# Eight raw-weight buffers in the down projections of a two-layer encoder, with the residual x kept in HBM meanwhile

## The chip, the cores and the metric

One core of a Trainium2 chip runs the whole program. The metric is device time in microseconds (us) of one execution, the median of several runs. A profiled execution gives a trace of every engine: TensorE (PE, with its weight loads as PEld), VectorE (DVE), ScalarE (ACT), GpSimd (POOL) and SyncE (SP), whose queue issues nearly all the DMAs here.

## The reference

A trunk of two layers on x of 256 tokens by 2048 features, all in float32. Each layer is a token mixer (attention) and a ConvGLU feed-forward, each with a norm before and after:

```
def conv_glu(h, w_up, conv_w, conv_b, w_down):
    u = h @ w_up
    gate, val = u[..., :D_FF], u[..., D_FF:]
    gate = depthwise_conv3(gate, conv_w, conv_b)
    return (jax.nn.gelu(gate, approximate=False) * val) @ w_down
...
        x = x + rms_norm(m, p['mix_post'])
        h = rms_norm(x, p['ffn_pre'])
        x = x + rms_norm(conv_glu(h, *p['ffn']), p['ffn_post'])
```

D_FF is 5632, so `w_down` is 5632 by 2048: 46 MB per layer. The change concerns `@ w_down` of both layers and the x that is added after it.

## The kernel before, in words

**Weights as a stream of chunks.** Every weight that the program needs is cut into chunks of 128 partitions by 1024 float32 (512 KB), listed once in the order of their use (`all_chunks`). `_load` (L122) takes a buffer with the tag `raw`, of which there are four, and issues the DMA on SP. `_split` (L130) makes of a raw chunk two matmul operands in float32r: ACT casts it (L149, the high part `whi`), DVE subtracts the high part from the raw one (L144, the rest `wlo`). Once DVE has done that, the raw buffer is free. `whi` and `wlo` have five buffers each. `weights()` (L163) hands out the next chunk; it splits up to the chunk after next and then asks for three loads more. A product of float32 precision is the sum of three float32r matmuls: high weight by high and by low activation (L1269, L1270 in the down projection), low weight by high activation (L1272).

**The order on each engine.** The code is written as one program with generators that are ticked between chunks (`now`, `tick`). A scheduler of the framework then lays out each engine's instructions in a fixed order, and puts in the waits. SP works through its queue in that order: an instruction that waits holds up all behind it.

**The feed-forward** (`ffn`, L1072). The up projection takes 176 chunks. Beside it `block_sums` (L1124) loads parts of `w_down`, forms differences of their blocks on DVE (L1130) and writes them back to HBM (tiles `b..`); they are used instead of plain blocks in a scheme that needs seven block products instead of eight (Strassen's). Its tiles are `st` and `g_last`.

**The down projection** (`down`, L1157) works in two halves h of 1024 output columns. Its list of items (`down_order`, L41) mixes two kinds. A *plain* item is one chunk of 512 KB with 12 matmuls. A *pair* p is four items j = 0 to 3: three chunks of 512 KB with 6 matmuls each (those of j = 1 and 2 come from the blocks in HBM, tile `b`) and one of 256 KB with 3. Half 0 has 9 pairs, half 1 has 11. In half 0, and in half 1 for the first three pairs, two plain items stand among a pair's items; from the fourth pair of half 1 on, one. The pairs' other operands are sums of tokens' blocks, made by `sums` (L1169) on DVE and ACT and kept in the tiles `seven`. Their homes are tiles that nothing else needs at that time: `xm0`, `xm1`, `xm2` (the input of the up projection), `st`, `gw`, `yf`, `misc`. In half 1 the temporary of `sums` itself takes a `raw` buffer.

After the last pair of each half, `done` adds up the results on DVE (tiles `m`, L1160), squares them on ACT (L331) and multiplies by the gains, which are loaded by `gain_row` (L420, tile `gb`, on SP). The last five plain items of half 1 are held back: all five are split first and then multiplied for one block of tokens and for the other (`HELD`). Then comes `crossing` (L446), which updates x and starts the next layer's mixer, or in layer 1 `tail` (L597), which writes the result.

The residual x lies in four tiles `x0` to `x3` of 128 by 1024 float32 for the whole program. In `ffn` they are read by `pre_norm` (L337) at its start, and then not before `crossing` or `tail`.

Of the kernel before, what the change touches and what calls it, by code (L numbers as in the profile page):

```python
# [2 lines left out]

# [1 line left out]

# [4 lines left out]
F32 = mybir.dt.float32  # L10
# [6 lines left out]
P = 128  # L17
# [40 lines left out]
class Model:  # L58
# [6 lines left out]
    def __init__(self, ctx, tc, a, out):  # L65
        self.tc, self.nc, self.a, self.out = tc, tc.nc, a, out
        self.soon, self.bg, self.running = [], deque(), []
        self.held = deque()
        self.gate, self.lead, self.led = (), None, 8
        pool = lambda name, **k: ctx.enter_context(tc.tile_pool(name=name, **k))  # L70
        self.const = pool("const", bufs=1)
        self.act = pool("act", bufs=1)
        self.wp = pool("wp", bufs=1)
        self.small = pool("small", bufs=2)
        self.ps = pool("ps", bufs=4, space=bass.MemoryType.PSUM)
        self.dram = pool("dram", bufs=1, space=bass.MemoryType.DRAM)
        self.blocks = {}


    def now(self, gen, after=()):  # L80
# [41 lines left out]
    def _load(self, i):  # L122
        if i >= len(self.chunks) or i in self.loaded or i < self.at or i in self.made:
            return
        src = self.chunks[i]() if callable(self.chunks[i]) else self.chunks[i]
        raw = self.wp.tile([P, 1024], F32, tag="raw", name="raw", bufs=4)[:, :src.shape[-1]]
        self.nc.sync.dma_start(out=raw, in_=src)
        self.loaded[i] = raw

# [33 lines left out]
    def weights(self, upto=None):  # L163

        i = self.at
        if upto is None:
            upto = i + (2 if self.lead else 3)
            self.follow()
        for j in range(i, upto):
            self._split(j)  # L170
        for j in range(upto, i + 6):
            self._load(j) if j < upto + 4 else None
        self.at += 1
        return self.made.pop(i)

# [896 lines left out]
    def ffn(self, layer, pre):  # L1072
        nc, tc = self.nc, self.tc
        with tc.tile_pool(name=f"ffn{layer}", bufs=1) as sp:
            self.room = sp
            xs = self.xhl
            x = lambda k: xs[k // 4][:, k % 4].rearrange("p a t -> p (a t)")
            gh = [sp.tile([P, 4, T], F32R, tag=f"gh{i}", name=f"gh{i}") for i in range(NFG - 1)]
            gl = [sp.tile([P, 4, T], F32R, name=f"gl{i}") for i in range(NFG - 1)]
            cw = lambda j, c: self.gain(f"l{layer}_conv_w", j * KF + c)  # L1080
            gw = sp.tile([P, 4, T], F32, tag="gw", name="gw", bufs=1)
            misc = sp.tile([P, 4, T], F32, tag="misc", name="misc", bufs=1)
            self.rb = misc[:, 0]
            norm = self.now(self.pre_norm(sp))
            blocks = None
            for gi in range(NFG):
                if gi == 1:
                    blocks = self.now(self.block_sums(layer, sp))
                pg = self.proj_t(KD, x, "acc", ROWS[layer] if gi == 0 else 0, gi == 0)
                self.finish(norm)  # L1090
                act = sp.tile([P, 4, T], F32, tag="yf", name="yf", bufs=1)

                def gates(ins=None, gi=gi, pg=pg, act=act):
                    for i in range(4):
                        c = 4 * gi + i
                        g = self.joined(gw[:, 2 + i % 2], gw[:, i % 2], pg[i])
                        if ins and i == 0:
                            with self.behind([ins]):
                                self.spread(sp)
                        y = act[:, i]  # L1100
                        nc.vector.tensor_tensor(out=g, in0=g, in1=self.rb, op=ALU.mult)
                        nc.scalar.activation(y, g, AF.Identity, scale=cw(1, c), bias=self.gain(f"l{layer}_conv_b", c))
                        nc.vector.scalar_tensor_tensor(out=y[:, 1:], in0=g[:, :T - 1], scalar=cw(0, c), in1=y[:, 1:],
                                                       op0=ALU.mult, op1=ALU.add)
                        nc.vector.scalar_tensor_tensor(out=y[:, :T - 1], in0=g[:, 1:], scalar=cw(2, c),
                                                       in1=y[:, :T - 1], op0=ALU.mult, op1=ALU.add)
                        nc.scalar.activation(y, y, AF.Gelu)

                if gi:
                    gates()  # L1110
                pv = self.proj_t(KD, x, "at", after=None if gi else gates)
                if gi == NFG - 1:
                    self.finish(blocks)
                    both = sp.tile([P, 2, 4, T], F32R, tag="g_last", name="g_last", bufs=1)
                    gh.append(both[:, 0])
                    gl.append(both[:, 1])
                for i in range(4):
                    u = self.joined(gw[:, 2 + i % 2], misc[:, 2 + i % 2], pv[i])
                    nc.vector.tensor_tensor(out=u, in0=u, in1=self.rb, op=ALU.mult)
                    nc.vector.tensor_tensor(out=u, in0=u, in1=act[:, i], op=ALU.mult)  # L1120
                    self.parted(gh[gi][:, i, :], gl[gi][:, i, :], u)
            self.down(gh, gl, 2 * layer + 1, pre)

    def block_sums(self, layer, sp):  # L1124

# [28 lines left out]
                yield  # L1154
            old = (job, new)

    def down(self, gh, gl, post, pre):  # L1157

        nc = self.nc
        add = lambda out, a, b, op=ALU.add: nc.vector.tensor_tensor(out=out, in0=a, in1=b, op=op)  # L1160
# [2 lines left out]
        seven, m, gains = [], [], []  # L1163
        many = PAIRS[0 if pre else 1]

        homes = [(self.act, "xm0", 2), (self.act, "xm1", 2), (self.act, "xm2", 2), (self.room, "st", 2),
                 (self.room, "gw", 1), (self.room, "yf", 1), (self.room, "misc", 1)]

        def sums(upto, small=False):  # L1169

# [40 lines left out]
        def added(h, at):  # L1211

            p1, p5, p6, p7 = at
            x = m[h]
            nc.scalar.copy(x[:, 0, 0], p1)
            add(x[:, 1, 0], p6, x[:, 0, 0])
            yield
            add(x[:, 0, 1], p7, x[:, 1, 0])
            add(x[:, 1, 0], p5, x[:, 1, 0])
            yield  # L1220
            add(x[:, 1, 1], p5, x[:, 0, 1])
            yield
# [10 lines left out]
        def done(h, o, first=None):  # L1233
            if first:
                yield from first
            for t in range(2):
                self.square_sums(ss[:, t, 2 * h + o:2 * h + o + 1], total(h, o, t))
                yield
                scaled(h, o, t)
                yield  # L1240
# [4 lines left out]
        for h in range(2):  # L1245
            items = down_order(h, many[h])
            units = [n for n, item in enumerate(items) if item[0] == "seven"]
# [15 lines left out]
            def products(i, t, w):  # L1263
                group = []
                while used and used[0][1][:2] == (i, t):
                    q, (_, _, b, x, blk) = used.popleft()
                    group.append((banks[b], *x(), slice(512 * blk, 512 * blk + 512), q == first[b], q == last[b]))
                for bank, xh, xl, c, start, _ in group:
                    mm(bank, xh, w[0][:, c], start=start, stop=False, skip_group_check=loose)  # L1269
                    mm(bank, xl, w[0][:, c], start=False, stop=False, skip_group_check=loose)  # L1270
                for bank, xh, _, c, _, stop in group:
                    ins = mm(bank, xh, w[1][:, c], start=False, stop=stop, skip_group_check=loose)  # L1272
                return ins if group else None

            for i in range(n):
                if i == units[0]:
                    banks += [self.psum("at") for _ in range(4)]
                w = self.weights()
                while items[i][0] == "seven" and len(seven) <= items[i][1]:
                    self.tick()  # L1280
                for t in range(2):
                    products(i, t, w)
                self.tick()
                if i == units[-1]:
                    m.append(self.act.tile([P, 2, 2, 512], F32, tag="xm2" if h else "xm3", name=f"m{h}"))
                    if h:
                        gains.append(self.gain_row(post, 3))
                    ended = self.now(done(h, 0, added(h, banks[4:])))
# [153 lines left out]
```

## Time and profile before

| What | us |
| --- | --- |
| median of 3 runs | 2122.31 |
| lowest and highest | 2117.88, 2123.18 |
| the profiled execution's own time | 2115.0 |
| its span, first to last instruction | 2113.2 |
| down projection of layer 0 in the trace | 819.8 to 1082.2 |
| down projection of layer 1 in the trace | 1838.7 to 2104.8 |

The granted TensorE clock is 0.997 of full speed over the span. All times of the trace are counted from the span's start. In the tables by stretch a column gives the busy time of an engine and, as x with a number, the instructions that touch the stretch; PEclk is the granted clock, then comes the busy share of the 16 DMA engines and the GB/s that they moved. Matmuls are pipelined: one of 512 columns is shown with 0.39 us, but the next begins before it ends.

### The profile page before, as it was taken

The numbers are of one execution on the slowest core, as the hardware profiler recorded it, in microseconds if no ns is written. First come the engines' busy times: TensorE is split into PE (matmuls) and PEld (weight loads), VectorE is DVE, ScalarE is ACT, GpSimd is POOL, SyncE is SP. The second block draws the span as 40 slices with busy tenths as digits, with TensorE's granted clock in tenths as the row PEclk, the third lists the DMA queues.
The fourth block names the chain that finished last, engine by engine and source line by source line (L and its number), as shares of the span: only waits on it lengthen the run. The fifth ranks groups of instructions, "written<-read, shape, count | busy, mean of one in ns | idle before, by whom it ended". The sixth has DMA issues, their size and how long they took to land.

```text
span 2113.2 us, 29789 instructions
## 1 busy us (share of the span) xinstructions
PE 2061.7 (98%) x10882; PEld 1734.5 (82%) x10882; DVE 1561.4 (74%) x2388; ACT 1159.2 (55%) x1817; POOL 0.2 (0%) x4
## 2 busy tenths in 40 slices
PE   9999999999999999998999999999999999999987
PEld 7888888888888888776678998888888888887655
DVE  6876758887787768675587875797888866785756
ACT  7654546555455555554465654664555655554543
POOL 0000000000000000000000000000000000000000
PEclk9999999999999999999999999999999999999999
DMA  9545576898998666777755435698999866577774
GB/s 329 173 153 169 164 208 225 326 337 318 321 320 266 184 195 191 250 241 245 242 189 178 140 123 191 204 317 314 319 328 328 307 193 191 175 244 251 235 231 173
DMA packets 143284, 501.37 MB, mean 237 GB/s; under 512 B 15905, under 2 KB 16417, under 8 KB 143137
## 3 DMA queue, kind: packets, MB, share of 16 engines
q1 hardware_dynamic: 142848, 499.19, 71.0%
q8 instruction: 85, 1.39, 0.3%
q14 instruction: 63, 0.51, 0.1%
q10 hardware_dynamic: 288, 0.28, 0.0%
HBM read 455.36 MB, written 44.04 MB: 236 GB/s over the span
## 4 chain that ended last, share of the span: by engine, by line
PE 79%; DMA 12%; DVE 5%; ACT 3%; issue 1%; ACTq 0%; DVEq 0%; SPq 0%
PE ps L223 30%; PE ps L225 15%; PE ps L208 8%; PE ps L206 8%; PE ps L207 8%; DMA raw<-in_w_down 7%; DMA raw<-b 5%; DVE wlo L144 4%; ACT whi L149 2%; PE ps L1272 2%; PE ps L1269 2%; PE ps L1270 2%; PE ps L633 1%; PE ps L292 1%; DVE m L1160 1%
## 5 line engine op out<-in xcount | busy, mean ns | idle before, releaser
L144 DVE TENSOR_TENSOR wlo<-raw,whi 128x1024 fp32r<-128x1024 f32 (+1 forms) x780 | 924.8, 1193 | 415.9 <-ACT whi L149 402.6
L149 ACT CAST whi<-raw 128x1024 fp32r<-128x1024 f32 (+1 forms) x780 | 796.2, 1027 | 690.1 <-PE ps L223 156.2
L223 PE MATMUL ps<-xhl,whi 128*128 128x512 f32 x2752 | 952.6, 394 | 0.0
L225 PE MATMUL ps<-xhl,wlo 128*128 128x256 f32 x2752 | 757.5, 277 | 0.0
L223 PEld LDWEIGHTS ps<-xhl,whi 128*128 128x128 f32 x2752 | 513.9, 188 | 117.1
L225 PEld LDWEIGHTS ps<-xhl,wlo 128*128 128x128 f32 x2752 | 516.5, 188 | 2.6
L1269 PE MATMUL ps<-whi,gh 128*128 128x512 f32 x440 | 177.2, 403 | 24.7 <-ACT whi L149 21.7
L1270 PE MATMUL ps<-whi,gl 128*128 128x512 f32 x440 | 172.7, 392 | 0.0
L1272 PE MATMUL ps<-wlo,gh 128*128 128x512 f32 x440 | 146.5, 407 | 9.9 <-DVE wlo L144 6.9
L1130 DVE TENSOR_TENSOR blocks<-blocks 128x512 f32<-128x512 f32 (+1 forms) x120 | 103.6, 865 | 69.2 <-DMA blocks<-in_w_down 49.2
L206 PE MATMUL ps<-whi,xhl 128*128 128x512 f32 x336 | 132.3, 395 | 1.5 <-ACT whi L149 1.5
L1269 PEld LDWEIGHTS ps<-whi,gh 128*128 128x128 f32 x440 | 83.0, 189 | 59.1 <-ACT whi L149 39.0
L207 PE MATMUL ps<-wlo,xhl 128*128 128x512 f32 x336 | 131.4, 391 | 0.0
L208 PE MATMUL ps<-whi,xhl 128*128 128x512 f32 x336 | 130.9, 391 | 0.1
L1272 PEld LDWEIGHTS ps<-wlo,gh 128*128 128x128 f32 x440 | 79.6, 189 | 47.1 <-DVE wlo L144 33.5
L206 PE MATMUL ps<-whi,oh 128*128 128x512 f32 x256 | 100.3, 392 | 0.0
L207 PE MATMUL ps<-wlo,oh 128*128 128x512 f32 x256 | 99.7, 390 | 0.0
L208 PE MATMUL ps<-whi,ol 128*128 128x512 f32 x256 | 99.7, 389 | 0.0
L296 ACT COPY gw<-ps 128x256 f32<-128x256 f32 x176 | 62.3, 369 | 67.8 <-DVE gw L297 23.9
L1270 PEld LDWEIGHTS ps<-whi,gl 128*128 128x128 f32 x440 | 83.1, 189 | 16.1
L206 PEld LDWEIGHTS ps<-whi,xhl 128*128 128x128 f32 x336 | 63.1, 188 | 14.0 <-ACT whi L149 1.8
L208 PEld LDWEIGHTS ps<-whi,xhl 128*128 128x128 f32 x336 | 62.9, 188 | 13.8 <-DVE xhl L687 0.7
(229 smaller groups left out, 2209.8 us busy)
## 6 DMA issues: line engine op xcount, KB each, us to landing
raw<-in_w_up SPq DMA_DIRECT2D x352, 512.0 KB, 5.0
raw<-in_w_down SPq DMA_DIRECT2D x136, 512.0 KB, 4.7
raw<-in_w_in SPq DMA_DIRECT2D x88, 512.0 KB, 4.3
blocks<-in_w_down SPq DMA_DIRECT2D x80, 512.0 KB, 6.8
b<-blocks SPq DMA_DIRECT2D x80, 512.0 KB, 7.5
raw<-b SPq DMA_DIRECT2D x80, 512.0 KB, 6.4
raw<-in_w_out SPq DMA_DIRECT2D x64, 512.0 KB, 4.2
raw<-in_w_down SPq DMA_DIRECT2D x40, 256.0 KB, 4.5
```

The source lines that it names most:

```text
L144: return nc.vector.tensor_tensor(out=lo[:, s], in0=raw[:, s], in1=hi[:, s].bitcast(F32), op=ALU.subtract)
L149: self.nc.scalar.copy(hi[:, s], raw[:, s])
L206: mm(ps, lh, rh, start=start, stop=False)
L207: mm(ps, lh, rl, start=False, stop=False)
L208: return mm(ps, ll, rh, start=False, stop=stop)
L223: ins = mm(out[i], hi[:, s[kk]], x(k), start=k == 0, stop=False, skip_group_check=opening)
L225: ins = mm(out[i][:, :T], lo[:, s[kk]], x(k)[:, :T], start=False, stop=k == nk - 1, skip_group_check=opening)
L296: self.nc.scalar.copy(b, ps[:, T:])
L1130: nc.vector.tensor_tensor(out=x[:, a:a + n], in0=x[:, b:b + n] if n > 512 else x[:, a:a + n], in1=x[:, a:a + n] if n > 512 else x[:, b:b + ...
L1269: mm(bank, xh, w[0][:, c], start=start, stop=False, skip_group_check=loose)
L1270: mm(bank, xl, w[0][:, c], start=False, stop=False, skip_group_check=loose)
L1272: ins = mm(bank, xh, w[1][:, c], start=False, stop=stop, skip_group_check=loose)
```

## The change

Two kinds of SBUF space get a second use during `down`.

- `_load` takes turns among eight buffers there: the four `raw` ones, and the tiles `x2`, `yf`, `x3` and `misc`, under the name `raw_more`. `weights()` asks for loads up to nine chunks ahead instead of five. Six items before the last pair's end in half 1 the list `self.more` is emptied, so that loads use the four `raw` buffers again.
- `x0` and `x1` become the first homes of the tokens' sums, one pair each; `yf` and `misc` are homes no more.
- x therefore leaves SBUF: after the first column group of the up projection four DMAs of 512 KB on SP write it to HBM (tile `x_kept`), and at the last item of half 1's last pair four DMAs read it back (`x_back`).

```
-        raw = self.wp.tile([P, 1024], F32, tag="raw", name="raw", bufs=4)[:, :src.shape[-1]]
+        turn = next(self.turns) % (4 + len(self.more))
+        if turn < len(self.more):
+            pool, tag = self.more[turn]
+            raw = pool.tile([P, 1024], F32, tag=tag, name="raw_more", bufs=1)
+        else:
+            raw = self.wp.tile([P, 1024], F32, tag="raw", name="raw", bufs=4)
+        raw = raw[:, :src.shape[-1]]
         self.nc.sync.dma_start(out=raw, in_=src)
...
-        for j in range(upto, i + 6):
-            self._load(j) if j < upto + 4 else None
+        for j in range(upto, i + 6 + len(self.more)):
+            self._load(j) if j < upto + 4 + len(self.more) else None
...
                 if gi == 1:
+                    kept = self.dram.tile([4, P, 2, 512], F32, name=f"x_kept{layer}")
+                    for c in range(4):
+                        nc.sync.dma_start(out=kept[c], in_=self.x[c])
                     blocks = self.now(self.block_sums(layer, sp))
...
-        homes = [(self.act, "xm0", 2), (self.act, "xm1", 2), (self.act, "xm2", 2), (self.room, "st", 2),
-                 (self.room, "gw", 1), (self.room, "yf", 1), (self.room, "misc", 1)]
+        homes = [(self.act, "x0", 1), (self.act, "x1", 1), (self.act, "xm0", 2), (self.act, "xm1", 2),
+                 (self.act, "xm2", 2), (self.room, "st", 2), (self.room, "gw", 1)]
+        self.more = [(self.act, "x2"), (self.room, "yf"), (self.act, "x3"), (self.room, "misc")]
+
+        def x_back():
+            for c in range(4):
+                self.x[c] = self.act.tile([P, 2, 512], F32, name=f"x{c}")
+                nc.sync.dma_start(out=self.x[c], in_=kept[c])
...
             for i in range(n):
+                if h and i == units[-1] - 6:
+                    self.more = []
+                if h and i == units[-1]:
+                    x_back()
```

The order of TensorE's instructions is the same. On ACT and DVE the sums of the first two pairs are cut in two, and the last ones come earlier. On SP the queue changes in three places. (In the rows a line number of the kernel stands first; those of the changed kernel are 8 to 21 higher: L135 is the load of a chunk, L1098 the store of x, L1184 its way back, L428 the gain row.)

The first place is SP at the start of layer 0's up projection, before:

```order
L127 DMA raw<-in_w_up 128x1024 x7
L420 DMA gb<-in_post 128x512
L127 DMA raw<-in_w_up 128x1024 x3
L1143 DMA blocks<-in_w_down 128x1024
L127 DMA raw<-in_w_up 128x1024
L1143 DMA blocks<-in_w_down 128x1024 x2
```

and now:

```order
L428 DMA gb<-in_post 128x512
L1098 DMA x_kept_3681<-x_296 128x1024
L1098 DMA x_kept_3681<-x_320 128x1024
L135 DMA raw<-in_w_up 128x1024
L1098 DMA x_kept_3681<-x_344 128x1024
L135 DMA raw<-in_w_up 128x1024 x3
L1098 DMA x_kept_3681<-x_370 128x1024
L1154 DMA blocks<-in_w_down 128x1024 x2
```

The four stores of x stand among the 8th to 11th chunk of the up projection, two of them ahead of the 8th, and the first blocks come behind them.

The second place is SP in layer 0's half 1, from the third to the fifth pair (`b_2` to `b_4`; an integer at a name's end only tells tiles apart), before:

```order
L127 DMA raw<-b_2_5967 128x1024 x2
L127 DMA raw<-in_w_down 128x1024
L127 DMA raw<-in_w_down 128x512
L127 DMA raw<-in_w_down 128x1024 x2
L127 DMA raw<-b_3_6163 128x1024 x2
L127 DMA raw<-in_w_down 128x512
L127 DMA raw<-in_w_down 128x1024 x2
L127 DMA raw<-b_4_6354 128x1024 x2
```

and now:

```order
L135 DMA raw<-b_2_5972 128x1024 x2
L135 DMA raw<-in_w_down 128x1024
L135 DMA raw_more<-in_w_down 128x512
L135 DMA raw_more<-in_w_down 128x1024 x2
L135 DMA raw_more<-b_3_6168 128x1024
L135 DMA raw<-b_3_6168 128x1024
L135 DMA raw<-in_w_down 128x512
L1184 DMA x_9735<-x_kept_3681 128x1024
L135 DMA raw<-in_w_down 128x1024 x2
L135 DMA raw_more<-b_4_6359 128x1024 x2
```

The loads come in the same order, four in `raw` and four in `raw_more` by turns, and the first quarter of x is read back here already: the scheduler has moved it up, and the second quarter (not shown) to just behind the sixth pair's first chunk. Both stand behind loads that cannot be issued before PE is through with the first and the second pair, whose sums their tiles held.

The third place is SP at the end of layer 0's half 1, before:

```order
L127 DMA raw<-b_10_7485 128x1024 x2
L127 DMA raw<-in_w_down 128x512
L127 DMA raw<-in_w_down 128x1024 x7
L127 DMA raw<-in_w_in 128x1024 x7
```

and now:

```order
L135 DMA raw<-b_10_7490 128x1024 x2
L135 DMA raw_more<-in_w_down 128x512
L135 DMA raw_more<-in_w_down 128x1024 x2
L135 DMA raw<-in_w_down 128x1024 x4
L1184 DMA x_9739<-x_kept_3681 128x1024
L1184 DMA x_9741<-x_kept_3681 128x1024
L135 DMA raw<-in_w_down 128x1024
L135 DMA raw<-in_w_in 128x1024 x7
```

The other two quarters of x stand ahead of the last chunk of `w_down` and of the next layer's first chunks. Their tiles `x2` and `x3` held the chunks of the last pair's last item and of the second plain item behind it, so each waits for that chunk's split.

More of the change, by code (lines that the diff above doesn't have):

```diff
@@ L2 @@
 from contextlib import ExitStack
+from itertools import count
 import numpy as np
@@ L77, in __init__ @@
         self.blocks = {}
+        self.more, self.turns = [], count()
     def now(self, gen, after=()):
@@ L1121, in ffn @@
                     self.parted(gh[gi][:, i, :], gl[gi][:, i, :], u)
-            self.down(gh, gl, 2 * layer + 1, pre)
+            self.down(gh, gl, 2 * layer + 1, pre, kept)
     def block_sums(self, layer, sp):
@@ L1155, in block_sums, with down @@
             old = (job, new)
-    def down(self, gh, gl, post, pre):
+    def down(self, gh, gl, post, pre, kept):
         nc = self.nc
```

## The prediction

> **What bounds the kernel now.** I read the page first, then the tables by stretch through both down projections, then who waits there, the chain of waits and the landing times of one stretch.
>
> ```profile
> span 2113.2 us, 29789 instructions
> PE 2061.7 (98%) x10882; PEld 1734.5 (82%) x10882; DVE 1561.4 (74%) x2388; ACT 1159.2 (55%) x1817; POOL 0.2 (0%) x4
> ```
>
> PE looks full at 98%, but its time per matmul is the pipelined one, so a slack PE still looks busy. The number of matmuls in a stretch tells more. By stretch, with PE's busy time and count first, and the granted clock, the DMA share and GB/s last:
>
> ```profile
> 830.00:860.00 30.00, 30.00 (x134) 24.82 (x134) 28.28 (x38) 17.30 (x19) 0.00 (x0) 1.00 0.78 239
> 820.00:870.00 50.00, 50.00 (x222) 41.36 (x222) 44.43 (x64) 29.07 (x35) 0.00 (x0) 1.00 0.67 212
> 870.00:940.00 70.00, 68.12 (x287) 52.43 (x285) 44.45 (x43) 36.75 (x41) 0.00 (x0) 1.00 0.81 262
> 940.00:964.00 24.00, 20.74 (x84) 15.23 (x85) 19.26 (x29) 14.13 (x20) 0.00 (x0) 1.00 0.68 209
> 964.00:1060.00 96.00, 87.26 (x343) 61.20 (x342) 53.98 (x50) 46.47 (x50) 0.00 (x0) 1.00 0.76 244
> 1060.00:1077.00 17.00, 13.86 (x53) 10.38 (x52) 15.19 (x21) 11.01 (x16) 0.00 (x0) 0.90 0.79 262
> 1889.00:1959.00 70.00, 66.36 (x278) 50.99 (x278) 41.26 (x39) 35.77 (x40) 0.00 (x0) 1.00 0.78 253
> 1959.00:1980.00 21.00, 17.39 (x72) 12.80 (x71) 18.71 (x31) 12.30 (x18) 0.00 (x0) 1.00 0.64 204
> 1980.00:2078.00 98.00, 88.20 (x342) 61.89 (x341) 54.60 (x51) 47.55 (x51) 0.00 (x0) 0.98 0.75 238
> 2078.00:2104.00 26.00, 21.78 (x86) 16.57 (x85) 18.55 (x28) 8.55 (x13) 0.00 (x0) 0.93 0.37 136
> ```
>
> A matmul counts where it touches a stretch, so the first row gives a pitch of (30 + 0.39)/134 = 0.227 us at full flow. What a stretch lost is its length plus 0.39 less 0.227 times its count. In layer 0 that is 0.0 for 820 to 870, then 5.2 (the rest of half 0), 5.3 (the changeover between halves), 18.5 (half 1's pairs) and 5.4 (its end), 34.4 us together; in layer 1 7.3, 5.0, 20.8 and 6.9, 40.0 us together. So some 74 us are to be had. In the longest stretch of layer 0 these waited (engine, for whom: us, times, longest; last SP's queue):
>
> ```profile
> ACT whi L149 <- DMA raw<-in_w_down: 22.4, 17, 2.3
> ACT whi L149 <- DMA raw<-b: 18.0, 15, 3.2
> PEld ps L1269 <- ACT whi L149: 14.4, 17, 1.7
> SPq L127 <- DVE wlo L144: 69.1, 50, 2.4
> ```
>
> PE waits for the cast, the cast for the load, and SP, which should issue the load, waits 69 of 96 us for DVE to free a raw buffer. That is a ring, and the chain of waits of that stretch, by line, goes round in it: 57% in loads, 28% in L144 and L149.
>
> ```profile
> by line: DMA raw<-b 32.4%; DMA raw<-in_w_down 24.2%; DVE wlo L144 15.7%; ACT whi L149 12.1%; PE ps L1269 5.4%; PE ps L1270 4.6%; PE ps L1272 4.4%; issue 2.6%; ACTq L149 0.4%; DVEq L144 0.1%
> L144 DVE TENSOR_TENSOR wlo<-raw,whi 128x1024 fp32r<-128x1024 f32 (+1 forms) x50 | 55.0, 1117 | 41.0 <-ACT whi L149 38.4 <-PE ps L1272 2.2
> L149 ACT CAST whi<-raw 128x1024 fp32r<-128x1024 f32 (+1 forms) x49 | 46.7, 970 | 50.0 <-DMA raw<-in_w_down 22.4 <-DMA raw<-b 18.0 <-PE ps L1270 6.4
> raw<-in_w_down SPq DMA_DIRECT2D x23, 512.0 KB, 4.6
> raw<-b SPq DMA_DIRECT2D x18, 512.0 KB, 6.5
> raw<-in_w_down SPq DMA_DIRECT2D x9, 256.0 KB, 5.5
> ```
>
> One turn of a buffer takes the mean landing, (23 x 4.6 + 18 x 6.5 + 9 x 5.5)/50 = 5.45 us, and a cast and a subtraction, 0.97 + 1.12: 7.5 us. Four buffers give a chunk every 1.9 us, and the stretch indeed took 96/50 = 1.92 us per chunk. PE at full flow needs five chunks (2.36 MB) per 33 matmuls, one every 1.50 us, or 315 GB/s. The ring of four is the bound.
>
> **The change part by part.** *Four more buffers.* Eight buffers at 1.50 us allow a turn of 12.0 us, of which 2.1 are the split: loads may land after 9.9 us instead of 3.9. Whether the DMAs then carry 315 GB/s is the next question. This stretch of the up projection is the nearest row:
>
> ```profile
> 440.00:480.00 40.00, 40.00 (x233) 34.96 (x232) 35.94 (x57) 22.65 (x35) 0.00 (x0) 1.00 0.91 331
> ```
>
> They moved 331 GB/s at a share of 0.91, so some 364 at a full one (my estimate from this row). Half 1's pairs need 315, and with the two early quarters of x (1.05 MB in about 60 us) 333, or 91% of that. It is tight, but seven chunks of stock, about 10 us of PE's work, cover swings. DVE's five splits for a group are 5 x 1.12 = 5.6 of PE's 7.5 us, ACT's casts less, so both go on hiding behind PE. I count 90% of the loss of the pairs as won: 0.9 x (5.2 + 7.3) = 11.2 and 0.9 x (18.5 + 20.8) = 35.4 us. The bounds are 100% and what a rival below leaves.
>
> *The changeover.* SP stands still there for the gain rows (first row), and PE for a bank that DVE's additions free (second row):
>
> ```profile
> SPq L420 <- DVE m L1160: 4.3, 1, 4.3
> PE ps L1269 <- DVE m L1160: 1.3, 1, 1.3
> ```
>
> The first wait stays, but eight buffers cover 4.3 us, and the gain rows stand some chunks later. The second stays, at about 2 us per layer with its weight load. Won: 10.3 - 4 = 6.3 us, between 0 and 8.
>
> *The end of half 1.* DVE's fixed order puts six additions and gains between two splits (layer 1, DVE, then PE):
>
> ```profile
> 2086.26 1.22 DVE L144 TENSOR_TENSOR wlo<-raw,whi 128x1024 fp32r<-128x1024 f32 x1
> 2087.39 2.48 DVE L1160 TENSOR_TENSOR m<-ps,m 128x512 f32<-128x512 f32 x4
> ...
> 2091.76 2.35 DVE L144 TENSOR_TENSOR wlo<-raw,whi 128x1024 fp32r<-128x1024 f32 x2
> ```
>
> ```profile
> 2093.03 1.22 PE L1272 MATMUL ps<-wlo,gh 128*128 128x512 f32 x2 [3.84 <-DVE wlo L144]
> ```
>
> The fifth of the seven last chunks is thus split at 2093.0, and PE stands until then. That order stays; but it began late, since the splits ahead of it waited for loads. With early loads DVE starts about 0.8 us after the last pair, has seven additions and gains and two splits to do, some 7.6 us, and is through at 8.4. PE by then has two plain items (12 matmuls, 2.72 us each) and two of the held ones for one block of tokens (6 matmuls, 1.36 us each) behind it and needs that split two thirds into the next, at 9.1. I count 8 of 12.3 us as won, between 3 and 12. In both last stretches the clock column stands under 1: 17 us at 0.90 are 1.7 us lost, which this sum holds. The Trainium skill, TensorE: Matmul & The Clock Gate, What's actually happening, says that PE's clock is halved after an idle window of about 3.4 us and stays so for at least another. The trace agrees: a mean of 0.90 over 17 us is one window of 3.4 us at half. By that rule a stall at the end that stays, but gets shorter than a window, gives back its 1.7 us all the same.
>
> *x leaves and returns.* The four stores of a layer take at most 4 x 512 KB at 331 GB/s, 6.3 us of DMA time. The first two can go once x is updated, and SP issues its next chunk later than that anyway (DVE, then SP):
>
> ```profile
> 330.21 1.42 DVE L455 SCALAR_TENSOR_TENSOR x<-m,postr,x 128x512 f32<-128x512 f32 x2
> 334.63 5.27 SPq L127 DMA_DIRECT2D raw<-in_w_up  x3
> ```
>
> So the queue isn't held up. The 8th chunk, issued at 334.63, is needed after four chunks more of PE's work (about 11 us); this is the cover, and without it each store would cost 1.6 us. I take 0.5 us per layer, between 0 and 6.3. The first two reloads are in the 333 GB/s above. The last two stand ahead of the last chunk of `w_down` and make it 3.2 us later; it is needed 5.4 + 4 x 1.36 = 10.9 us after the last pair, and its load is early by then. Again 0.5 us per layer, between 0 and 3.2. A gain is excluded, since they only add traffic.
>
> *The sums.* Cutting the first two in halves adds a few short instructions where PE lost nothing (820 to 870); DVE has 5.6 us left there. Nothing; about 1 us if it hadn't. `yf` and `misc` are read last by DVE here:
>
> ```profile
> 826.43 0.76 DVE L682 TENSOR_TENSOR g_last<-misc,g_last 128x256 fp32r<-128x256 f32 x2
> ```
>
> The loads into them, and all behind, wait until 827.2 in layer 0. The earliest chunk so placed is the seventh of layer 1, which PE reaches 15 us after the stage's start and which can be issued after 8: nothing.
>
> *The sum.* 11.2 + 35.4 + 6.3 + 8.0 - 2.0 = 58.9 us, from 2115.0 to 2056.1 for an execution like the profiled one. The median of the runs is 7.3 us above that one, so I predict 2122.3 - 58.9 = 2063.4 us, say 2063.
>
> **The rivals.** *The DMAs become the bound.* For it: loads from `b` land after 6.5 us against 4.6, so blocks may be slow to read, and no stretch of the down projections exceeds 262 GB/s. Against it: DMA share there is 0.64 to 0.81, and 4 buffers can't ask for more. With 275 GB/s in the pairs, half 1's 23.4 MB (96 us at 244) and 1.05 MB more would take 88.9 us, a gain of 7.1; layer 1's 98 us become 88.7, a gain of 9.3; half 0's stretches gain 3.3 and 5.6. With 7 us at changeovers and ends and 2 us of costs: 2122.3 - 30.3 = 2092.
>
> *It costs time.* If loads land later just as they get more, so that the down projections keep their 244 GB/s, nothing is won and 2.1 MB of reloads come on top of a stage that the DMAs bound: 8.6 us per layer, 2139 us. It decides below 244 x (1 + 2.1/23.4) = 266 GB/s in half 1. For it: landing times with one to three loads in flight are already above this row of the up projection without blocks (min, median, max):
>
> ```profile
> DMA to landing us min/median/max: 3.2/4.2/4.6
> ```
>
> Against it: the same engines carry 331 GB/s with blocks and stores beside the weights.
>
> *The buffers are not what is short.* A lone load lands in 3.2 us; with that, four buffers turn in 5.3 us and feed 1.3 us per chunk, and PE's loss would come from elsewhere, or the scheduler's queue wouldn't issue the loads earlier: 2122 us. The 1.92 us per chunk, which the ring gives to 2%, speaks against it. The Trainium skill, DMA: Bandwidth & Descriptors, Anatomy of one DMA, has about 2.0 us plus the bytes at 436 GB/s for the path that GpSimd issues, 3.2 us for 512 KB, and by it four buffers would suffice as well. The trace agrees for a lone load only, not for those of the ring.
>
> **How the numbers follow.** Forecast 0.75; DMAs the bound 0.12; no effect 0.03; slower 0.05; all 74 us won, below 2050, 0.05. The forecast's own range is 2050 to 2080: at the low end all losses but one wait at each changeover are won (-72), at the high end 90% becomes 70% and the costs reach 6 us. To hold 8 in 10, with something kept back for what I don't see, the range is 2050 to 2092. A measurement of this kernel can tell about 0.3% (6 us) from no change. Faster 0.91 (forecast, all won, most of the DMA rival), same 0.04, slower 0.05.
>
> **What would show it.** Right: in half 1 SP's wait for L144 falls to a small part, the stretch's DMA rate rises to about 315 to 335 GB/s at a share over 0.9, and its 343 matmuls take about 80 us; DVE's additions at the end start before 1 us has passed and no stall of 3 us follows; the clock stays at 1.00 there. Wrong: landing times over 10 us with PE still waiting for casts (the DMAs are the bound), PE waiting in the up projection's first 40 us (the stores cost), or SP waiting long at the reloads of x (L1184).

## The result, and the profile after

| | us |
| --- | --- |
| before, median of 4 runs (2112.36 to 2123.18) | 2120.1 |
| after, median of 4 runs (2060.65 to 2063.37) | 2063.2 |
| ratio, 95% interval | 0.973, 0.9705 to 0.9763 |
| profiled execution after: own time, span | 2060.65, 2058.9 |
| down projections after, layer 0 and layer 1 | 832.2 to 1059.0, 1823.9 to 2050.1 |

The change makes the kernel 2.7% faster, at the time that was predicted; that the number fits is luck, as is shown below. The stretches of the down projections that answer to those shown of before (PE's busy time and count first; clock, DMA share and GB/s last):

```profile
882.00:946.00 64.00, 64.00 (x285) 53.01 (x284) 45.97 (x46) 36.98 (x42) 0.00 (x0) 1.00 0.87 291
946.00:966.00 20.00, 20.00 (x90) 16.58 (x89) 15.94 (x21) 14.05 (x19) 0.00 (x0) 1.00 0.82 256
966.00:1044.00 78.00, 78.00 (x346) 64.63 (x345) 57.12 (x56) 48.10 (x53) 0.00 (x0) 1.00 0.90 312
...
1956.00:2034.00 78.00, 78.00 (x346) 64.62 (x345) 54.88 (x51) 47.39 (x51) 0.00 (x0) 1.00 0.91 308
2034.00:2051.00 17.00, 16.49 (x70) 12.55 (x69) 14.24 (x25) 4.93 (x10) 0.00 (x0) 1.00 0.25 92
```

By the formula of the prediction (length plus 0.39 less 0.227 times the count) these lost nothing: 78 + 0.39 - 0.227 x 346 is -0.2. Half 1's pairs took 96 us for 343 matmuls before and take 78 for 346 now. The clock stands at 1.00 at the end too, where it was 0.90 and 0.93. Who still waits in the pairs of layer 0, all rows, and behind that SP's first row for 960 to 1040:

```profile
ACT whi L157 <- PE ps L1287: 29.2, 39, 2.1
DVE wlo L152 <- ACT whi L157: 18.4, 19, 1.8
```

```profile
SPq L135 <- DVE wlo L152: 54.9, 47, 2.6
```

No wait of PE is left, and none of ACT for a load: ACT waits for PE now, to hand back a cast's buffer. SP still waits 55 of 80 us for a raw buffer, though. A queue that runs ahead of its user always ends up waiting for a free buffer; that wait alone doesn't tell a ring that bounds from one that is full.

From its first matmul's start to its last one's, a down projection takes 226.8 and 226.2 us; before, it took 262.0 and 265.7 (819.8 to 1081.8, 1838.7 to 2104.4). That is 35.2 + 39.5 = 74.7 us won. The span fell by 2113.2 - 2058.9 = 54.3 us only: layer 0's down projection starts 12.4 us later, and from its last matmul to the first one of layer 1's it is 764.9 us instead of 756.9. These 20.4 us were lost in the two up projections. The same stretch of layer 0, before and then after:

```profile
580.00:660.00 80.00, 80.00 (x463) 69.95 (x463) 69.34 (x109) 43.38 (x67) 0.00 (x0) 1.00 0.91 320
```

```profile
580.00:660.00 80.00, 76.42 (x420) 65.20 (x419) 61.19 (x95) 39.35 (x61) 0.00 (x0) 0.98 0.90 310
```

This is where `block_sums` works beside the up projection (the block phase). DVE and PE waited there, from 480 to 660 us, for these (the rows of before are the first fence; PE has none in it):

```profile
DVE blocks L1130 <- DMA blocks<-in_w_down: 17.6, 5, 6.0
DVE blocks L1130 <- DMA raw<-in_w_up: 3.3, 1, 3.3
```

```profile
DVE blocks L1141 <- DMA blocks<-in_w_down: 18.3, 7, 4.2
DVE blocks L1141 <- DMA raw<-in_w_up: 8.1, 2, 4.3
DVE blocks L1141 <- issue: 7.8, 2, 6.2
PEld ps L233 <- DVE wlo L152: 6.7, 7, 2.7
PE ps L233 <- DVE wlo L152: 4.5, 5, 2.4
```

DVE, which works in order, stands 34.2 us at block sums whose data isn't there, instead of 20.9, and the splits that PE needs stand behind them. SP's queue from 440 to 660 us, before and after, at its block loads (L1143, L1154) and block stores (L1149, L1160):

```profile
SPq L1143 <- DMA b<-blocks: 15.6, 6, 4.3
SPq L1149 <- DVE blocks L1130: 0.9, 1, 0.9
```

```profile
SPq L1154 <- DMA b<-blocks: 16.3, 5, 8.0
SPq L1160 <- DMA blocks<-in_w_down: 8.2, 3, 3.5
SPq L1160 <- DVE blocks L1141: 6.1, 3, 2.1
```

SP now comes to stores of blocks before their sums are made, and stands there for 14.3 us with weight loads behind it. The longest wait of PE, and what stood before it on SP and DVE:

```profile
625.99 0.42 SPq L1154 DMA_DIRECT2D blocks<-in_w_down  x1
```

```profile
633.24 1.23 DVE L1141 TENSOR_TENSOR blocks<-blocks 128x1024 f32<-128x1024 f32 x1 [3.66 <-DMA blocks<-in_w_down]
...
637.30 1.22 DVE L152 TENSOR_TENSOR wlo<-raw,whi 128x1024 fp32r<-128x1024 f32 x1
```

```profile
638.57 0.53 PE L233 MATMUL ps<-xhl,wlo 128*128 128x256 f32 x1 [2.38 <-DVE wlo L152]
```

The block load that SP issued at 625.99 us landed at 633.2. DVE stood 3.66 us at the block sum that needs it, went through the instructions that its order has behind that sum, and came to the split only at 637.30, although the cast of that chunk was done by 631.0. PE waited for this split. After that SP stands for 8 us, from 630.3 to 638.4, at the next block load, which waits until the store just ahead of it has landed, and issues no weights; no wait of PE follows from this (from 640 to 830 us there is none). Just ahead of that block load stand two early loads of the down projection, at 629.16 and 629.98 us: x2 and x3 are free as soon as they are stored, so the scheduler may issue the first loads into them some 200 us before their use.

### The profile page after: what moved, and what is told of

Its sections match the earlier page's. It is cut to its first block, busy times and chain, and to the rows that moved or that the text cites. A ratio compares the mean times of both kernels' runs of the same rounds, so it can differ in the third digit from the quotient of the medians.

```text
span 2058.9 us, 29791 instructions
## 1 busy us (share of the span) xinstructions
PE 2037.1 (99%) x10882; PEld 1746.5 (85%) x10882; DVE 1560.2 (76%) x2388; ACT 1156.4 (56%) x1817; POOL 0.2 (0%) x4
## 4 chain that ended last, share of the span: by engine, by line
PE 87%; DVE 5%; DMA 4%; issue 2%; ACT 1%; SPq 0%; DVEq 0%; ACTq 0%
PE ps L231 25%; PE ps L233 12%; PE ps L216 8%; PE ps L214 8%; PE ps L215 8%; PE ps L1287 7%; PE ps L1286 7%; PE ps L1289 7%; DMA blocks<-in_w_down 3%; DVE wlo L152 2%; PE ps L641 1%; PE ps L300 1%; DMA raw<-in_w_up 1%; DVE blocks L1141 1%; PE ps L544 1%
## 5 line engine op out<-in xcount | busy, mean ns | idle before, releaser
L152 DVE TENSOR_TENSOR wlo<-raw,whi 128x1024 fp32r<-128x1024 f32 (+1 forms) x663 | 793.7, 1205 | 298.7 <-ACT whi L157 292.2
L157 ACT CAST whi<-raw 128x1024 fp32r<-128x1024 f32 (+1 forms) x663 | 682.9, 1036 | 520.7 <-PE ps L231 184.2
L233 PEld LDWEIGHTS ps<-xhl,wlo 128*128 128x128 f32 x2752 | 519.8, 189 | 15.6 <-DVE wlo L152 12.8
L1286 PE MATMUL ps<-whi,gh 128*128 128x512 f32 x440 | 171.5, 390 | 0.0
L152 DVE TENSOR_TENSOR wlo<-raw_more,whi 128x1024 fp32r<-128x1024 f32 (+1 forms) x117 | 130.7, 1132 | 48.6 <-ACT whi L157 43.8
L157 ACT CAST whi<-raw_more 128x1024 fp32r<-128x1024 f32 (+1 forms) x117 | 113.2, 979 | 77.2 <-PE ps L1287 70.0
L1289 PE MATMUL ps<-wlo,gh 128*128 128x512 f32 x440 | 138.8, 390 | 0.0
```

What stands on the lines that cost most here:

```text
L152: return nc.vector.tensor_tensor(out=lo[:, s], in0=raw[:, s], in1=hi[:, s].bitcast(F32), op=ALU.subtract)
L157: self.nc.scalar.copy(hi[:, s], raw[:, s])
L233: ins = mm(out[i][:, :T], lo[:, s[kk]], x(k)[:, :T], start=False, stop=k == nk - 1, skip_group_check=opening)
```

## The experiments

Three explanations of the 20.4 us were to be told apart. *Theory 1*: the stores of x make the scheduler lay out the block phase in another order on SP, and that order stalls DVE. *Theory 2*: the two early loads into x2 and x3 push the rest back. *A third*: the bytes of the stores and early loads cost it, wherever they are. The measurements of all runs together (excess is what a down projection took beyond full flow: of each step over 0.25 us from one of its matmuls' start to the next, the part beyond 0.227; SP's and DVE's waits for blocks are those of 440 to 660 and 480 to 660 us; each ratio is against runs of the kernel before made in the same rounds, whose medians are 2114.7 to 2120.1):

| kernel | median, us | ratio, 95% | SP at block stores | DVE at block sums | down 0 starts | down 0 to down 1 | excess, layers 0, 1 |
| --- | --- | --- | --- | --- | --- | --- | --- |
| before | 2120.1 | | 0.9 | 20.9 | 819.8 | 756.9 | 35.1, 38.5 |
| after | 2063.2 | 0.9705 to 0.9763 | 14.3 | 34.2 | 832.2 | 764.9 | 1.2, 0.6 |
| stores and reads of x, four buffers | 2141.0 | 1.0087 to 1.0135 | 17.0 | 29.5 | 832.6 | 768.5 | 39.7, 38.8 |
| early loads held back | 2060.0 | 0.9723 to 0.976 | 15.2 | 28.3 | 831.8 | 770.5 | 1.0, 0.3 |
| stores of x late | 2044.4 | 0.9637 to 0.9673 | 0.9 | 21.5 | 825.4 | 756.9 | 1.6, 0.0 |
| six buffers | 2041.8 | 0.9642 to 0.9679 | 0.9 | 20.7 | 819.9 | 757.7 | 1.4, 0.0 |
| five buffers | 2063.1 | 0.9728 to 0.9758 | 0.9 | 20.8 | 819.9 | 757.6 | 11.9, 10.2 |
| block stores held back | 2040.0 | 0.962 to 0.9649 | 0 | 6.0 | 819.9 | 757.0 | 1.1, 0.5 |
| stores of x by ScalarE | 2051.9 | 0.9672 to 0.9709 | 16.7 | 27.2 | 828.7 | 761.2 | 1.0, 0.3 |
| the hold alone, four buffers | 2115.5 | 0.9956 to 0.9999 | 0 | 3.7 | 820.1 | 756.9 | 36.8, 39.4 |
| the hold with six buffers | 2039.9 | 0.9617 to 0.9652 | 0 | 1.7 | 820.2 | 757.0 | 1.1, 0.0 |

**Stores and reads of x alone**, in the kernel before:

```diff
                 if gi == 1:
+                    kept = self.dram.tile([4, P, 2, 512], F32, name=f"x_kept{layer}")
+                    for c in range(4):
+                        nc.sync.dma_start(out=kept[c], in_=self.x[c])
...
+                if h and i == units[-1]:
+                    x_back()
```

> The kernel before, with the four stores of x to HBM at the second group of the up projections and the four reads back at the end of the down projections, but with four raw buffers and the old homes of the sums. Both down projections should flow as before (excess 35 and 38 us). Theory 1, the stores at the head of the block phase put SP's block loads, block stores and weight loads in another order and VectorE, which works in order, waits for late block loads: the up projections lose 8 to 16 us of the 20 that the changed kernel lost, total 2128 to 2137, ratio 1.004 to 1.008. Theory 2, the two loads into x2 and x3 that are issued in the middle of the block phase push the others back: nothing is lost here, ratio 0.999 to 1.001.

Theory 1's direction, and more than it gave: 1.1% slower than before, with 12.8 and 11.6 us lost in the up projections and 4.6 more in layer 0's down projection. It isn't quite the stores alone: the scheduler put two of the reads of x into the block phase too.

**The early loads held back**, in the changed kernel (`behind` makes the scheduler lay out an instruction behind those named):

```diff
-        self.nc.sync.dma_start(out=raw, in_=src)
+        with self.behind([self.last] if self.more else []):
+            self.last = self.nc.sync.dma_start(out=raw, in_=src)
```

> The changed kernel, with each raw load of the down projections held behind the raw load before it in SP's order, so that no load into x2 or x3 is issued in the block phase; the stores of x stay where they are. Theory 2 (those two loads push the others back): the jumps of 4.3 and 4.2 us at the end of the block phase go, with the drift behind them at most all 20 us; 2046 to 2055 us, ratio 0.965 to 0.969. Theory 1 (the order that the stores of x set): less than 3 us is won, ratio 0.972 to 0.974.

Theory 2 falls. The loads into x2 and x3 are gone from the block phase (the first one of layer 0 now comes at 831.7 us), and layer 0's loss is 12.0 instead of 12.4 us; layer 1's is 13.6 instead of 8.0.

**The stores of x late**, behind the block phase:

```diff
-        self.nc.sync.dma_start(out=raw, in_=src)
+        self.last = self.nc.sync.dma_start(out=raw, in_=src)
...
-                if gi == 1:
+                if gi == 9:
                     kept = self.dram.tile([4, P, 2, 512], F32, name=f"x_kept{layer}")
-                    for c in range(4):
-                        nc.sync.dma_start(out=kept[c], in_=self.x[c])
+                    with self.behind([self.last]):
+                        for c in range(4):
+                            nc.sync.dma_start(out=kept[c], in_=self.x[c])
+                if gi == 1:
                     blocks = self.now(self.block_sums(layer, sp))
```

> The changed kernel, with the four stores of x issued in the tenth group of the up projections, after the block phase, so that the block phase's order on SP is that of the kernel before, and the loads into x2 and x3 come after it too. Eight raw buffers in the down projections as in the changed kernel. Theories 1 and 2 both expect that the up projections lose nothing (under 3 us a layer) and the down projections keep their 226 us: about 2113 less 74.7 and plus 2 to 5, which is a total of 2042 to 2048, ratio 0.963 to 0.966. A third theory, that the bytes of the stores and of the early loads cost this wherever they stand, expects no change against the changed kernel, ratio 0.972 to 0.974.

As theories 1 and 2 had it, but for one thing. The bytes are all there, and most of the 20 us is back. Layer 0 still starts its down projection 5.6 us late, where under 3 were expected, without any wait of PE; the last section comes back to that.

**Six buffers**, two tiles of x stored:

```diff
-                    for c in range(4):
+                    for c in range(2):
                         nc.sync.dma_start(out=kept[c], in_=self.x[c])
...
-        self.more = [(self.act, "x2"), (self.room, "yf"), (self.act, "x3"), (self.room, "misc")]
+        self.more = [(self.room, "yf"), (self.room, "misc")]
...
-            for c in range(4):
+            for c in range(2):
                 self.x[c] = self.act.tile([P, 2, 512], F32, name=f"x{c}")
...
-                if h and i == units[-1] - 6:
+                if h and i == units[-1] - 4:
```

> Six raw buffers in place of eight: the two tiles of the up projections alone, which come free only at their end; x2 and x3 stay in SBUF, and x0 and x1 alone are stored and read back. By the ring's rule six turns at 1.50 us leave 9.0 us for landing, cast and subtraction, so landings up to 6.9 us are covered; the changed kernel's landings are 5.2 to 6.0 us on average. I expect an excess of 2 to 8 us in each down projection (before 35 and 38, with eight 1). The rival, that single landings scatter so far that eight are needed, gives an excess above 12 us each. The up projections: by theory 2 they lose nothing, by theory 1 half to all of what they lost. Total by ring's rule and theory 2: 2046 to 2058, ratio 0.965 to 0.971; with theory 1: 2055 to 2075, ratio 0.970 to 0.979.

Six do what eight do, and a little better than expected. Landings from 950 to 1032 us (of the issues, the 512 KB chunks of the down projection; each row ends with a median):

```profile
raw<-in_w_down SPq DMA_DIRECT2D x16, 512.0 KB, 6.2
raw<-b SPq DMA_DIRECT2D x12, 512.0 KB, 5.8
raw_more<-in_w_down SPq DMA_DIRECT2D x8, 512.0 KB, 5.8
raw_more<-b SPq DMA_DIRECT2D x4, 512.0 KB, 6.2
```

All these stay under the 6.9 us that six turns allow. Two stores of x, where four stood, don't upset the block phase.

**Five buffers**, the tile `yf` alone beside the four (the edit is against the kernel with six):

```diff
-        self.more = [(self.room, "yf"), (self.room, "misc")]
+        self.more = [(self.room, "yf")]
...
-                if h and i == units[-1] - 4:
+                if h and i == units[-1] - 3:
```

> Five raw buffers: the tile of the gates alone beside the four; x0 and x1 stored and read back, as with six. The ring's rule gives 7.5 us per turn with the landings of the kernel before (5.45 + 0.97 + 1.12), so 1.50 us a chunk, exactly what the products need: full flow on average, with nothing to spare for a landing that is late. I expect an excess of 4 to 14 us in each down projection (with four 35 and 38, with six 1.4 and 0.0), and no loss in the up projections: 2045 to 2066 us, ratio 0.967 to 0.977. If the rule is wrong and only the count of transfers in flight matters, the excess with five lies near half of that with four, 17 us or more each, ratio 0.979 or more.

The ring's rule holds to 6%. Landings, PE's waits (without a third row of 1.6 us) and the stretch, 952 to 1040 us:

```profile
raw<-in_w_down SPq DMA_DIRECT2D x25, 512.0 KB, 5.3
raw<-b SPq DMA_DIRECT2D x18, 512.0 KB, 5.9
raw_more<-in_w_down SPq DMA_DIRECT2D x9, 256.0 KB, 6.0
x<-x_kept SPq DMA_DIRECT2D x2, 512.0 KB, 7.0
```

```profile
PEld ps L1289 <- DVE wlo L152: 4.2, 10, 0.5
PEld ps L1286 <- ACT whi L157: 4.1, 6, 1.0
```

```profile
952.00:1040.00 88.00, 85.97 (x362) 66.42 (x361) 59.63 (x55) 51.67 (x55) 0.00 (x0) 1.00 0.88 296
```

By these medians the 52 landings of chunks average 5.63 us, with cast and subtraction 7.7: a fifth of it is 1.54 us per chunk, just above the 1.50 that PE needs. ACT cast 54 chunks in these 88 us, one every 1.63. PE's waits have turned from a few long ones into many of up to 1 us. Excess by buffers: four 35 and 38, five 12 and 10, six 1 and 0, eight 1 and 1 us.

**The block stores held back**, in the changed kernel, all four stores of x at their place:

```diff
-        self.nc.sync.dma_start(out=raw, in_=src)
+        self.last = self.nc.sync.dma_start(out=raw, in_=src)
...
-                    nc.sync.dma_start(out=half(kept, q - 2), in_=half(old[1], q - 2))
+                    with self.behind([self.last]):
+                        nc.sync.dma_start(out=half(kept, q - 2), in_=half(old[1], q - 2))
```

> The changed kernel with all four stores of x where they are, but each store of a block sum held behind the weight load that stands before it in the program, so that SP doesn't reach it before VectorE has made the sum. In the changed kernel SP waits 14.3 us at these stores between 440 and 660 us, in the kernel before 0.9. Theory 1a, the order on SP in the block phase is what costs the up projections their time: SP's waits at the block stores fall under 4 us, the up projections lose under 3 us a layer, 2042 to 2052 us, ratio 0.963 to 0.968. Theory 1b, the stores' own transfers at that place cost it whatever the order: no change, ratio 0.972 to 0.974.

Theory 1a: the up projections lose nothing now (0.1 us in each layer), and the bytes and rows of the stores are the same. DVE's waits at the block sums, 480 to 660 us, and SP's at the block loads, 440 to 660:

```profile
DVE blocks L1141 <- DMA blocks<-in_w_down: 4.3, 2, 2.2
DVE blocks L1141 <- issue: 1.7, 2, 1.0
```

```profile
SPq L1154 <- DMA b<-blocks: 35.0, 12, 5.8
```

SP waits more than ever at the block loads, 35.0 us instead of 16.3, and PE waits for nothing from 480 to 660 us. The total of a queue's waits says little; what stands behind them decides. The hold moved more than the block stores: the two early loads of layer 0 now come at 360 and 410 us. That isn't what mended it, for in the next kernel they stand at 363 and 380 us and the loss is there. And DVE waits less here than in the kernel before, 6.0 us instead of 20.9, so a small cost of the bytes could hide in that slack.

**The stores of x issued by ScalarE**:

```diff
-                        nc.sync.dma_start(out=kept[c], in_=self.x[c])
+                        nc.scalar.dma_start(out=kept[c], in_=self.x[c])
```

> The changed kernel with the four stores of x issued by ScalarE at the same place of the program, so that they are on no row of SP; the bytes are the same and move at about the same time. The scheduler's order of the block phase is still not that of the kernel before: stores of two blocks stand next to each other. Theory 1a (order of the block phase): the up projections lose 4 to 12 us a layer here too, ratio 0.968 to 0.974. Theory 1c, the rows of the stores on SP hold back the weight loads behind them: no loss, ratio 0.963 to 0.966.

Theory 1a again, and not 1c: without a row of theirs on SP the up projections still lose 8.9 and 4.3 us, and SP again stands at the block stores:

```profile
SPq L1160 <- DMA blocks<-in_w_down: 9.7, 3, 3.9
SPq L1160 <- DVE blocks L1141: 7.0, 4, 2.1
```

In the table the four kernels in which SP waits 14 to 17 us there, and DVE 27 us or more at block sums, are those in which PE waits in the block phase; with DVE's 21.5 us or less PE doesn't.

**The hold alone**, in the kernel before, and **the hold with six buffers** (both edits as above):

> The kernel before, four raw buffers and x in SBUF, with each store of a block sum held behind the weight load that stands before it in the program; nothing else. Its up projections run at full flow already, and SP waits 0.9 us at these stores, so if the hold only mends an order that the stores of x spoil, nothing is won here: ratio 0.998 to 1.002, the down projections still with an excess of 35 and 38 us. If the hold wins something of its own, the ratio falls under 0.996.

> Six raw buffers with two tiles of x stored, and the hold on the stores of block sums. With six and the old order the up projections lost nothing and the down projections had an excess of 1.4 and 0.0 us, so nothing is left for the hold to win: 2038 to 2043 us, ratio 0.962 to 0.967, the same as with eight and the hold. If eight buffers give something that six don't, this is over 0.3% slower than that one (2040.0).

The hold alone gave 2115.5 against 2117.5 us, a ratio of 0.9977 (0.9956 to 0.9999), with the excess of four buffers in both layers: no clear gain of its own. With six buffers it gave 2039.9 us, 0.9634 (0.9617 to 0.9652), the same as with eight (2040.0). These two are the fastest versions, 1% under the changed kernel, and six buffers move half as much of x. Six buffers without the hold, at 2041.8, can't be told from them.

## Why the prediction was right

The time was right, 2063.4 worked out and 2063.2 measured, but by luck and not by its own sum. Three errors cancel: 13.8 us too little won, 18.4 us too little lost, and 4.8 us from the distance between the median and the profiled execution, taken as 7.3 from before and 2.5 after (2063.2 - 2060.65).

- *The ring of four is the bound*: right, and shown by the series of four, five, six and eight buffers. The estimate of 1.50 us per chunk for PE's need is borne out by five, which are just short of it, and six, which aren't.
- *The pairs*: 46.6 us were counted, 90% of what was lost. All was won. The rate is 308 to 312 GB/s at a share of 0.90 to 0.91, a little under the forecast (315 to 335 and over 0.9), and loads land after 6 to 7 us, far from the 9.9 that eight buffers allow (966 to 1044 us, the lowest and the highest row of 512 KB chunks):

```profile
raw_more<-in_w_down SPq DMA_DIRECT2D x8, 512.0 KB, 5.9
raw_more<-b SPq DMA_DIRECT2D x7, 512.0 KB, 6.7
```

- *The changeover*: 6.3 us counted, about 10 won. The step that failed is that PE's wait for a bank stays: no wait of PE stands between 946 and 966 us. SP's wait for the additions at the gain rows, which was to stay too, fell from 4.3 to 1.0 us. So DVE has the additions done in time; that this is because it no longer goes from load to load is likely but wasn't tested.
- *The end of half 1*: 8.0 counted, some 12 won. DVE's order is as it was said (layer 1; the fifth of the last splits is the first of the two at 2038.48):

```profile
2032.71 0.68 DVE L1171 TENSOR_TENSOR m<-ps,m 128x512 f32<-128x512 f32 x1
2033.35 1.23 DVE L152 TENSOR_TENSOR wlo<-raw,whi 128x1024 fp32r<-128x1024 f32 x1
2034.49 2.48 DVE L1171 TENSOR_TENSOR m<-ps,m 128x512 f32<-128x512 f32 x4
...
2038.48 2.35 DVE L152 TENSOR_TENSOR wlo<-raw,whi 128x1024 fp32r<-128x1024 f32 x2
```

  The last pair is through at about 2030.6. The additions start 2.1 us behind it instead of 0.8 (that sign of being right failed), and the fifth split ends at 2039.7, 9.1 us behind it instead of 8.4. That is when PE comes to it, as was worked out (9.1), so the stall of 3.84 us is gone with nothing to spare. The clock's 1.7 us came back, as said, but with the stall gone this is no test of the rule for a stall that stays; the last section has one, and there it fails.
- *The reloads of x and the early loads into `yf` and `misc`*: nothing, as said or nearly (1 us counted).
- *The stores of x*: this step failed, by its size and by its mechanism. 0.5 us a layer were counted, 6.3 at most; 12.4 and 8.0 were lost. The bound priced their bytes and their rows on SP at the place where they stand, 331 to 342 us, and the text looked for the harm in the up projection's first 40 us. PE waits for nothing there. The harm comes from 490 us on, some 140 us after these stores had landed, by way of the order that the scheduler gave to block loads, block stores and weight loads once four more instructions were in the queue. That order is fixed before the program starts. Which exchange in it does the harm, and why the scheduler makes it, stays open. That the order does it is shown by the kernel with the block stores held back, which moves the same bytes at the same place and loses nothing. The stores on ScalarE rule out only that their rows on SP do it.
- *What would show it*: "SP's wait for a raw buffer falls to a small part" was a wrong sign. It fell from 69 of 96 us only to 55 of 80.

Of the rivals, "all 74 us won" was true of the down projections, with 74.7, but not of the kernel. That the DMAs become the bound, or that landing times rise to eat the gain, is refuted by landings of 6 to 7 us with no wait of PE. That the buffers are not what is short is refuted by the series of four to six. (The 3.2 us taken there for a lone load is the shortest: twelve weight loads with no other DMA in flight beside them took 3.2 to 3.8 us in the trace of before.) Whether all eight buffers are needed was not asked, and six are enough.

## What to carry to other kernels

A ring of buffers feeds a chunk every (landing + time until it is emptied) / buffers. Work out the need of the consumer and take one buffer more than makes the two equal. Here that was six, and eight won nothing more, while they need twice as much of x moved. A few DMAs added to an in-order queue cost what they do to the order of everything behind them, in a list that a scheduler lays out, so compare the order of the whole stage, and look for an instruction that is reached before its data, with urgent loads behind it.

## What the runs showed of the hardware that was not expected

**A short stall can cost more than its length.** After PE's wait of 2.38 us at 638.57 in the changed kernel, by stretches, with the clock third from the end:

```profile
638.00:640.00 2.00, 1.43 (x5) 1.24 (x6) 2.00 (x5) 1.31 (x3) 0.00 (x0) 0.66 0.80 215
640.00:642.00 2.00, 2.00 (x8) 1.71 (x7) 2.00 (x3) 1.54 (x3) 0.00 (x0) 0.50 0.91 322
642.00:644.00 2.00, 2.00 (x13) 1.78 (x12) 2.00 (x3) 0.24 (x1) 0.00 (x0) 0.98 1.01 385
```

The clock is at half from the end of the wait to about 642.1, some 3.4 us, so that the 2.4 us cost about 4.1. The Trainium skill, TensorE: Matmul & The Clock Gate, What's actually happening, asks for an idle window of about 3.4 us; here a wait of 2.4 us was enough, and the half clock lasted for about one window. PE need not be idle for all of such a window, then: in the 3.41 us just before the half clock it was busy for 1.03.

```profile
635.24:638.65 3.41, 1.03 (x7) 0.63 (x5) 3.41 (x9) 2.39 (x5) 0.00 (x0) 1.00 1.00 402
```

Nor does the length of the wait decide alone. In the kernel with the stores and reads alone PE waited 2.88 us, up to 1679.22, and the clock stayed at 1.00. If that trace is cut into steps of 3.413 us, counted from the start of its half clock at 640.4, an edge at 1678.0 falls into this wait, and PE is busy for 0.50 of the step before and 0.66 of the one after. Cut so, all eleven traces agree while matmuls run: a step in which PE is busy for under 0.45 is followed by half clock, one with over 0.52 never, and between the two both happen.

**The up projection has two paces.** From 650 to 820 us PE is busy all the time at a full clock in both of these, before and after:

```profile
650.00:820.00 170.00, 170.00 (x983) 148.69 (x982) 120.61 (x191) 93.47 (x140) 0.00 (x0) 1.00 0.65 200
```

```profile
650.00:820.00 170.00, 170.00 (x964) 147.52 (x963) 119.49 (x192) 90.56 (x139) 0.00 (x0) 1.00 0.67 204
```

983 matmuls (with six buffers too) or 964: a pace that differs by 2%, and costs about 3.4 of the 12.4 us in this stretch. The changed kernel changes its pace at stalls, and in both directions: after one at 592 us it is slow, after one at 622 us it has the full pace again, and after the long wait it stays slow to the end of the stage. Two stretches of 10 us from it, the slow one first:

```profile
594.00:604.00 10.00, 10.00 (x58) 8.64 (x58) 5.38 (x7) 5.80 (x8) 0.00 (x0) 1.00 0.94 313
624.00:634.00 10.00, 10.00 (x60) 8.82 (x59) 6.05 (x9) 6.26 (x10) 0.00 (x0) 1.00 0.94 332
```

In the kernel with late stores the slow pace begins at about 545 us without a wait that the trace shows, and is the 5.6 us left there. Two of that kernel's five runs took 2040 us and three 2044 to 2046, so it may not come in every run; one of the three was traced. The cause stays open.
